# Four buffers instead of three for the weights, and sums over partitions formed as token columns

## The chip, the cores and the metric

One core of a Trainium2 chip runs the whole network in one launch. The metric is device time in microseconds, the median of the runs. All arithmetic is fp32 in and out; products run on TensorE (PE) as fp32r, three products for each fp32 one (below).

## The reference, cut to what matters

Two mixer layers (a gated mLSTM beside a sliding-window attention, then a squared-ReLU MLP), and an NSA attention layer behind them, on 512 tokens of width 1024:

```python
for l in range(2):
    h = rmsnorm(x, norm_mix_g[l])
    x = x + mixer_block(h, ...)        # mLSTM (4 heads) + windowed attention (16 heads)
    x = x + sqrelu_mlp(rmsnorm(x, norm_mlp_g[l]), w_up[l], w_down[l])
x = rmsnorm(x, final_norm_g)
u = rms_norm(x, pre_norm_gain)
x = x + rms_norm(nsa_mixer(u, ...), post_norm_gain)   # compressed, selected, windowed branch

def rmsnorm(x, g):
    y = x * lax.rsqrt(jnp.mean(x * x, axis=-1, keepdims=True) + EPS)
    return y * g
```

Every norm needs, for each token, a sum over the 1024 features. The mLSTM needs two such sums for each head (the denominator and the squares of the numerator), and the running maximum of its gates on all 128 partitions.

## The kernel before

Activations lie with features on the 128 partitions and tokens along the row, in eight tiles of 128x512. A product of the network is `gemm`: one 128x1024 weight tile of 512 KB, split into a high part `wh` and a low part `wl`, times eight pairs `xgh`, `xgl`; that is 24 matmuls of 512 columns (`mm3`: high by high, low by high, high by low). `gemm_tok` (tile `gt`) does the same with tokens on the output's partitions.

`wload` brings a weight tile: SyncE (SP) issues the DMA into `raw`, ScalarE (ACT) copies it to `wh`, VectorE (DVE) subtracts to get `wl`; in the NSA part GpSimd (POOL) does every second subtraction. `RB` buffers stand for `raw`, `WB` for each of `wh` and `wl`: three each. All other 128x512 tiles come from one pool of `U_SLOTS` = 79.

The code doesn't run in the order in which it is written. A `Recorder` notes every operation, and `issue` puts them in order with a list scheduler: it goes through time with a price for every operation (`cost`, and `load` for PE's weight loads), gives out buffers as they come free, and takes the earliest ready operation on each engine. The engines then run their queues strictly in that order. All operations are emitted from one helper line, L346, so that rows of the profile are told apart by their tiles' names.

Sums over partitions are made by `col_sums` (called 13 times: five norms through `stat_sum`, or directly in `nsa`, and eight mLSTM heads). Two matmuls with a selector of two columns as the stationary operand give a 2x512 row (`sums`, PSUM tag `o`), ACT copies it to SBUF (`sr`), four small transposes turn it into token columns (`sc`, PSUM tag `a`). `rsqrt` (DVE, then a power on POOL) and `bcast` (four transposes `bc`, an ACT copy) make of it a tile that scales columns. `mlstm_gates` writes the gates' maximum as rows 0 to 3 (high) and 32 to 35 (low) of `Mr`, and each `mlstm_head` spreads its row over the partitions with one matmul of 36 partitions (`bc<-Mr,selh`).

The scheduler's order in three places is in the section on the change. PSUM has four banks of tag `g` and two each of `a` and `o`.

Of the kernel before, what the change touches and what calls it, by code (L numbers as in the profile page):

```python
# [7 lines left out]
F32 = mybir.dt.float32  # L8
F32R = mybir.dt.float32r
AF = mybir.ActivationFunctionType  # L10
# [8 lines left out]
NB = T // 128  # L19
# [27 lines left out]
PE, ACT, DVE, POOL, SP = range(5)  # L47
# [12 lines left out]
def _free(ap):  # L60
    n = 1
    for _, c in ap.ap[1:]:
        n *= c
    return n


def _psum(ap):
    return "PSUM" in str(ap.space)
# [16 lines left out]
class Recorder:  # L85
# [14 lines left out]
    @staticmethod  # L100
    def cost(eng, name, out, wide, scalars, kw):

        n = _free(out)
        if eng == PE:
            return n * 0.4428 * (4 if name == "matmul" and wide[0].dtype == F32 else 1), False
        if eng == ACT:
            return 192 + 0.842 * n - (22 if _psum(wide[0]) else 0) + 88 * min(scalars, 2), False
        if eng == DVE:
            both = sum(1 for x in wide if not _psum(x)) > 1
            if name == "tensor_reduce":  # L110
                n = _free(wide[0])
            if name == "reciprocal":
                return 140 + 8 * n, both
            if name == "tensor_tensor_scan":
                return 1209, both
            if name in ("tensor_copy", "tensor_scalar") and not _psum(wide[0]):
                return 150 + n / 1.92 + 60 * scalars, n > 4
            return 148 + 1.05 * n + 60 * scalars, both
        if eng == POOL:
            if name == "memset":  # L120
                return 100 + 0.8 * n, False
            if kw.get("op") == ALU.pow:
                return 230 + 197 * n, True
            return (100 if name == "tensor_copy" else 170) + 2.2 * n, True
        return 60, False
# [26 lines left out]
    def add(self, eng, name, fn, args, kw):  # L152
        op = Op()
        op.eng, op.fn, op.args, op.kw, op.dma = eng, fn, args, kw, name == "dma_start"
        aps = [x for x in args if isinstance(x, bass.AP)]
        outs = [kw["out"]] if "out" in kw else [aps.pop(0)]
        ins = aps + [v for k, v in kw.items() if isinstance(v, bass.AP) and k not in ("out", "accum_out")]
        out = outs[0]
        wide = [x for x in ins if _free(x) > 1 or _free(out) == 1]
        single = [x for x in ins if not (_free(x) > 1 or _free(out) == 1)]  # L160
        op.cost, op.port = self.cost(eng, name, out, wide, len(single), kw) if not op.dma else (60, False)
        op.load = 0.8333 * _free(ins[0]) if eng == PE else 0
        op.acc = kw.get("accum_out") is not None
        op.reads = op.writes = None
        if eng in GAP:
            op.writes, op.reads = self.place(out), [self.place(x) for x in wide + single]
        if op.acc:
            outs.append(kw["accum_out"])
        i = len(self.ops)
        preds, tiles = {}, set()  # L170
        for w, ap in [(False, x) for x in ins] + [(True, x) for x in outs]:
            t, r = self.region(ap)
            if t in self.tag and self.tag[t][1]:
                tiles.add(t)
            keep, psum = [], t in self.tag and self.tag[t][0] in ("g", "a", "o")
            for q, qw, qr in self.hist.setdefault(t, []):
                hit = r is None or qr is None or (r[0] < qr[1] and qr[0] < r[1] and r[2] < qr[3] and qr[2] < r[3])
                if q != i and hit and (w or qw or psum and self.ops[q].eng != eng):
                    preds[q] = preds.get(q, False) or qw
                if not (w and hit and r is not None and qr is not None and r[0] <= qr[0] and r[1] >= qr[1]  # L180
                        and r[2] <= qr[2] and r[3] >= qr[3]):
                    keep.append((q, qw, qr))
            keep.append((i, w, r))
            self.hist[t] = keep
        for t in tiles:
            if t not in self.users:
                self.users[t] = 0
                self.first.append(t)
            self.users[t] += 1
        op.preds, op.npred, op.succs, op.tiles, op.rt = preds, len(preds), [], tiles, 0  # L190
        for q in preds:
            self.ops[q].succs.append(i)
        self.ops.append(op)
# [164 lines left out]
class Net:  # L358
# [97 lines left out]
    def col_sums(self, *xs):  # L456

        z, sel = xs[0], self.ones2r
        if len(xs) == 2:
            z, sel = self.u("hz"), self.sel2  # L460
            for n, x in enumerate(xs):
                self.tt(z[n * 64:n * 64 + 64], x[:64], x[64:], ALU.add)
        zh, zl = self.split(z, None, "sq")
        rows = self.ps("o", "sums")
        self.mm(rows[:2], sel, zh, True, False)
        self.mm(rows[:2], sel, zl, False, True)
        r = self.u("sr")
        self.nc.scalar.activation(r[:2], rows[:2], AF.Copy)
        ps = self.ps("a", "sc")
        for b in range(NB):  # L470
            self.tp(ps[:, 2 * b:2 * b + 2], r[:2, b * 128:(b + 1) * 128], 2)
        return ps

    def stat_sum(self, acc):
# [36 lines left out]
    def consts(self):  # L511
        nc, a = self.nc, self.a
        c = lambda n, name, dt=F32: nc.tile(self.cp, [128, n], dt, name, name, 1)
        self.ident = c(128, "ident")
        nc.sync.dma_start(self.ident, a["ident"])
        self.jrev = c(128, "jrev")
        nc.vector.tensor_copy(rev(self.jrev[:, :]), self.ident)
        self.bc = c(48, "bc")
        nc.sync.dma_start(self.bc, bass.AP(tensor=a["brow"].tensor, offset=a["brow"].offset,
                                             ap=[[0, 128], [1, 48]]))  # L520
        self.maskn = c(128, "maskn")
        nc.sync.dma_start(self.maskn, a["maskn"])
        self.masku = c(128, "masku")
        nc.sync.dma_start(self.masku, a["masku"])
        self.ones2r = c(2, "ones2r", F32R)
        nc.gpsimd.memset(self.ones2r.bitcast(F32), 1.0)
        self.mhalf = c(16, "mhalf")
        nc.gpsimd.memset(self.mhalf, -0.5)
        self.ones4 = nc.tile(self.cp, [4, T], F32, "ones4", "ones4", 1)
        nc.gpsimd.memset(self.ones4, 1.0)  # L530
        z = c(2, "z2")
        nc.gpsimd.memset(z, 0.0)
        for n in range(2):
            nc.gpsimd.memset(z[64 * n:64 * n + 64, n:n + 1], 1.0)
        self.sel2 = c(2, "sel2", F32R)
        nc.vector.tensor_copy(self.sel2, z)

        self.selh = nc.tile(self.cp, [36, 512], F32R, "selh", "selh", 1)
        col = lambda n: self.ident[:36, n:n + 4, None].to_broadcast([36, 4, 128])
        self.tt(self.selh.rearrange("p (h c) -> p h c", h=4), col(0), col(32), ALU.add)  # L540
        self.nsink = c(32, "nsink")
        nc.vector.tensor_scalar(self.nsink, self.bc[:, :32], -1.0, None, op0=ALU.mult)
        self.gmh = c(16, "gmh")
        nc.vector.tensor_scalar(self.gmh, self.pc[:, PC_GM:PC_GM + 16], 0.5, None, op0=ALU.mult)
        self.gfp = c(8, "gfp")
        self.tt(self.gfp, self.pc[:, PC_GFIN:PC_GFIN + 8], self.pc[:, PC_PRE:PC_PRE + 8])
# [315 lines left out]
    def mlstm_gates(self, gt):  # L862


        nc = self.nc
# [5 lines left out]
        z = self.sm("z", 16)  # L871
# [20 lines left out]
        for b in range(NB):  # L892
            c = slice(b * 128, (b + 1) * 128)
# [14 lines left out]
        nc.vector.tensor_scalar(fl, pcol[:, 16:32], -1.0, 85.0, op0=ALU.mult, op1=ALU.min)  # L908
        nc.scalar.activation(fl, fl, AF.Exp)
        Mr = self.u("Mr", F32R)  # L910
        nc.gpsimd.memset(Mr[:36].bitcast(F32), 0.0)
        nc.scalar.activation(Mr[:4], M[:4], AF.Copy)
        self.tt(Mr[32:36], M[:4], Mr[:4].bitcast(F32), ALU.subtract)
        return Ac, Mr, fl
# [1 line left out]
    def mlstm_head(self, h, q, k, V, vc, gates):  # L916
        nc = self.nc
        Ac, Mr, fl = gates
        pm, nMb = self.ps("a", "bc"), self.u("nMb")
        self.mm(pm, self.selh[:, h * 128:h * 128 + 128], Mr[:36], True, True)  # L920
        nc.scalar.activation(nMb, pm, AF.Copy, scale=-1.0)
        nMd = self.u("nMd")
        self.tt(nMd.rearrange("p (b t) -> p b t", b=NB), nMb.rearrange("p (b t) -> p b t", b=NB),
# [2 lines left out]
        for j in range(NB):  # L926
            c = slice(j * 128, (j + 1) * 128)
            n = T - j * 128
            ps = self.ps("a", "ST")
# [14 lines left out]
        for v in range(2):  # L944
            o = self.ps("o", "num")
# [18 lines left out]
        r = self.rsqrt(t, 1.0 / 256)  # L964
# [395 lines left out]
        self.nsa(x_dram, xs, st[0], st[1], out)  # L1360


U_SLOTS, SM_SLOTS, WB, RB = 79, 32, 3, 3
POOL_LO, WARM, WINDOW = 2, 7, 500
RESERVE = {"u": 8, "sm": 8, "a": 99, "o": 99, "g": 99, "raw": 99, "wh": 99, "wl": 99}

# [106 lines left out]
```

## Time and profile before

| what | us |
|---|---|
| median of 3 runs | 2156.1 (2155.67 to 2156.34) |
| the profiled execution | 2155.65 |
| its span, first to last instruction | 2153.9 |
| PE matmuls busy | 2131.5 (99%) |
| PE weight loads busy (beside the matmuls) | 1776.9 (83%) |
| DVE, ACT, POOL busy | 1371.9, 1063.6, 425.2 |
| granted TensorE clock, mean over the span | 0.997 |

A matmul's end is modelled in the profile, so that a busy share says little of PE; the distance from one matmul's start to the next one's start is what it costs. Both 1.2 and 2.4 GHz occur: a granted clock of 1.00 is 2.4 GHz. "Idle" in brackets is the time in which the engine did nothing just before the instruction, with the one that ended it.

### The profile page before, as it was taken

What the parts mean: (1) busy time and instruction counts of PE and PEld (TensorE: products, weight loads), DVE (VectorE), ACT (ScalarE), POOL (GpSimd) and SP (SyncE); (2) the same over time, 40 slices, a digit from 0 to 9 for tenths busy, and PEclk for the clock granted to TensorE, in tenths of its full rate; (3) what the DMA queues carried; (4) which work ended last, traced back from release to release, by engine and by line L of the source; (5) the groups of instructions that cost most, each with busy time, mean ns of one, the idle gap of its engine ahead of it and who ended that gap; (6) DMA issues with size and microseconds to landing.
All of it is one profiled execution on the core that took longest, in us unless ns stands there. A gap on an engine that the chain in (4) does not pass through costs nothing.

```text
span 2153.9 us, 28049 instructions
## 1 busy us (share of the span) xinstructions
PE 2131.5 (99%) x10389; PEld 1776.9 (83%) x10389; DVE 1371.9 (64%) x2587; ACT 1063.6 (49%) x2066; POOL 425.2 (20%) x470
## 2 busy tenths in 40 slices
PE   8999999999999999999999999999999999999998
PEld 6888888888888888888888888888888888888877
DVE  6688995444343445668998444434435677888786
ACT  5466773234232334456675223322324457787783
POOL 3133441011000002014453002000000404232311
PEclk9999999999999999999999999999999999999999
DMA  5223223432333333322322333333333352232231
GB/s 159 83 67 99 79 84 98 127 98 89 97 98 98 98 98 118 98 79 79 99 79 79 123 104 99 96 98 98 98 99 113 108 166 89 69 81 60 86 98 40
DMA packets 72425, 206.08 MB, mean 96 GB/s; under 512 B 9760, under 2 KB 18592, under 8 KB 72288
## 3 DMA queue, kind: packets, MB, share of 16 engines
q1 hardware_dynamic: 72288, 204.30, 30.8%
q8 instruction: 81, 1.33, 0.2%
q14 instruction: 56, 0.46, 0.1%
HBM read 197.85 MB, written 6.42 MB: 95 GB/s over the span
## 4 chain that ended last, share of the span: by engine, by line
PE 94%; DVE 2%; POOL 1%; issue 1%; DMA 1%; ACT 1%; SPq 0%; DVEq 0%; POOLq 0%; ACTq 0%
PE g L346 75%; PE gt L346 5%; PE S L346 3%; PE O L346 3%; PE PT L346 2%; PE num L346 1%; PE go L346 1%; PE ST L346 1%; DVE wl L346 0%; POOL vb L346 0%; PE bc L346 0%; POOL sq L346 0%; PE sums L346 0%; DMA raw<-wn 0%; PE sc L346 0%
## 5 line engine op out<-in xcount | busy, mean ns | idle before, releaser
L346 ACT ACTIVATE wh<-raw 128x1024 fp32r<-128x1024 f32 (+2 forms) x344 | 355.5, 1034 | 757.8 <-PE g L346 573.3
L346 PE MATMUL g<-xgh,wl 128*128 128x512 f32 x1512 | 596.2, 394 | 4.2 <-DVE wl L346 2.2
L346 PE MATMUL g<-xgh,wh 128*128 128x512 f32 x1512 | 595.6, 394 | 2.4 <-ACT wh L346 1.4
L346 PE MATMUL g<-xgl,wh 128*128 128x512 f32 x1512 | 595.2, 394 | 0.4 <-DVE xgl L346 0.4
L346 DVE TENSOR_TENSOR wl<-raw,wh 128x1024 fp32r<-128x1024 f32 (+2 forms) x327 | 409.5, 1253 | 121.0 <-ACT wh L346 119.2
L346 PEld LDWEIGHTS g<-xgh,wl 128*128 128x128 f32 x1512 | 285.0, 188 | 61.2 <-DVE wl L346 3.3
L346 PEld LDWEIGHTS g<-xgh,wh 128*128 128x128 f32 x1512 | 285.1, 189 | 58.6 <-ACT wh L346 2.4
L346 PEld LDWEIGHTS g<-xgl,wh 128*128 128x128 f32 x1512 | 284.9, 188 | 56.7 <-DVE xgl L346 1.9
L346 POOL TENSOR_TENSOR sq<-sq 128x512 f32<-128x512 f32 x50 | 83.4, 1669 | 592.3 <-ACT sq L346 581.0
L346 PE MATMUL g<-hidh,wh 128*128 128x512 f32 x512 | 199.2, 389 | 0.0
L346 PE MATMUL g<-hidh,wl 128*128 128x512 f32 x512 | 199.2, 389 | 0.0
L346 PE MATMUL g<-hidl,wh 128*128 128x512 f32 x512 | 199.2, 389 | 0.0
L346 DVE TENSOR_TENSOR x<-x,g 128x512 f32<-128x512 f32 x80 | 55.0, 688 | 207.1 <-PE g L346 207.1
L346 DVE SCALAR_TENSOR_TENSOR hz<-g,Rb 128x512 f32<-128x512 f32 x64 | 44.3, 692 | 157.8 <-PE g L346 151.8
L346 ACT ACTIVATE L<-L,mn 128x256 f32<-128x256 f32 (+3 forms) x256 | 131.2, 513 | 24.2 <-DVE mn L346 22.1
L346 PEld LDWEIGHTS g<-hidl,wh 128*128 128x128 f32 x512 | 96.1, 188 | 20.0
L346 PEld LDWEIGHTS g<-hidh,wl 128*128 128x128 f32 x512 | 96.1, 188 | 19.9
L346 PEld LDWEIGHTS g<-hidh,wh 128*128 128x128 f32 x512 | 96.1, 188 | 19.9
L346 DVE TENSOR_TENSOR pl<-PT,ph 128x512 fp32r<-128x512 f32 (+1 forms) x160 | 78.8, 525 | 22.7 <-ACT ph L346 22.0
L346 PE MATMUL gt<-wh,xgh 128*128 128x512 f32 (+3 forms) x256 | 87.8, 344 | 0.0
L346 PE MATMUL gt<-wh,xgl 128*128 128x512 f32 (+3 forms) x256 | 87.5, 342 | 0.0
L346 PE MATMUL gt<-wl,xgh 128*128 128x512 f32 (+3 forms) x256 | 87.3, 343 | 0.0
(307 smaller groups left out, 3698.2 us busy)
## 6 DMA issues: line engine op xcount, KB each, us to landing
raw<-wf SPq DMA_DIRECT2D x258, 512.0 KB, 3.5
raw<-wn SPq DMA_DIRECT2D x41, 512.0 KB, 3.7
raw<-wmv SPq DMA_DIRECT2D x16, 512.0 KB, 3.7
x<-x SPq DMA_DIRECT2D x16, 256.0 KB, 4.0
bt<-E SPq DMA_DIRECT2D x16, 256.0 KB, 5.1
xsp<-x SPq DMA_DIRECT2D x16, 256.0 KB, 2.0
raw<-w SPq DMA_DIRECT2D x8, 512.0 KB, 4.0
bn<-E SPq DMA_DIRECT2D x16, 256.0 KB, 4.9
```

The costliest lines, as they stand in the source:

```text
L346: op.fn(*op.args, **op.kw)
```

## The change

- `WB` and `RB` go from 3 to 4, `U_SLOTS` from 79 to 80. The room comes from the scratch for dynamic DMAs at the start of SBUF, which is set to 1024 bytes per partition.
- `col_sums` takes the data as the stationary operand: four 128x128 blocks of the high part, then four of the low part, each with the two-column selector as the moving operand, accumulated straight into token columns (`sums<-sel2,sqh`, PSUM tag `a`). The row in SBUF and the small transposes are gone.
- `selh` and `Mr` have 128 partitions in place of 36, the new rows being zero.
- The scheduler's price for a transpose becomes 0.844 ns per column (0.4428), and 0.42 ns for its weight load (0.8333).

```diff
-            return n * 0.4428 * (4 if name == "matmul" and wide[0].dtype == F32 else 1), False
+            return n * (0.844 if name == "transpose" else 0.4428 if wide[0].dtype == F32R else 1.771), False
...
-        op.load = 0.8333 * _free(ins[0]) if eng == PE else 0
+        op.load = (0.42 if name == "transpose" else 0.8333) * _free(ins[0]) if eng == PE else 0
...
-        zh, zl = self.split(z, None, "sq")
-        rows = self.ps("o", "sums")
-        self.mm(rows[:2], sel, zh, True, False)
-        self.mm(rows[:2], sel, zl, False, True)
-        r = self.u("sr")
-        self.nc.scalar.activation(r[:2], rows[:2], AF.Copy)
-        ps = self.ps("a", "sc")
-        for b in range(NB):
-            self.tp(ps[:, 2 * b:2 * b + 2], r[:2, b * 128:(b + 1) * 128], 2)
+        ps = self.ps("a", "sums")
+        for n, y in enumerate(self.split(z, None, "sq")):
+            for b in range(NB):
+                self.mm(ps[:, 2 * b:2 * b + 2], y[:, b * 128:(b + 1) * 128], sel, n + b == 0, n == 1)
...
-        self.selh = nc.tile(self.cp, [36, 512], F32R, "selh", "selh", 1)
-        col = lambda n: self.ident[:36, n:n + 4, None].to_broadcast([36, 4, 128])
+        self.selh = c(512, "selh", F32R)
+        col = lambda n: self.ident[:, n:n + 4, None].to_broadcast([128, 4, 128])
...
-        nc.gpsimd.memset(Mr[:36].bitcast(F32), 0.0)
+        nc.gpsimd.memset(Mr.bitcast(F32), 0.0)
...
-        self.mm(pm, self.selh[:, h * 128:h * 128 + 128], Mr[:36], True, True)
+        self.mm(pm, self.selh[:, h * 128:h * 128 + 128], Mr, True, True)
...
-U_SLOTS, SM_SLOTS, WB, RB = 79, 32, 3, 3
+U_SLOTS, SM_SLOTS, WB, RB = 80, 32, 4, 4
...
-    nc = bacc.Bacc("TRN2", target_bir_lowering=False, num_devices=1)
+    nc = bacc.Bacc("TRN2", target_bir_lowering=False, num_devices=1, dynamic_dma_scratch_size=1024)
```

Buffers and prices both feed the scheduler, so the whole order changes. Three places. The numbers behind the names are buffers' and differ between the two kernels.

PE's queue in the first layer, at the first sum over partitions, before (`gt` is the token-major product for the attention's values, with one accumulator for each of four token blocks; the first `gt` of all stands 17 rows above `sums`):

```order
L346 MATMUL gt_146<-wh_153,xgl_91 128x264
L346 MATMUL gt_145<-wl_154,xgh_90 128x264
L346 MATMUL sums_131<-sqh_129,ones2r_120 2x512
L346 MATMUL gt_147<-wh_150,xgh_81 128x264
L346 MATMUL gt_147<-wh_150,xgl_82 128x264
```

The same place after:

```order
L346 MATMUL gt_146<-wh_148,xgh_87 128x264
L346 MATMUL gt_146<-wh_148,xgl_88 128x264
L346 MATMUL gt_146<-wl_149,xgh_87 128x264
L346 MATMUL sums_129<-ones2r_120,sqh_130 128x2 x4
L346 MATMUL gt_143<-wh_151,xgh_90 128x264
```

The first `gt` now stands 24 rows above the first `sums`. Before, `sums` took a bank of tag `o`, and the third block (`gt_147`, of the same tag) came only behind it.

DVE's queue at the start of the NSA layer, before (`v` and `gate` evict the finished `gt`; `wl_2922` is the low part of the weights of the key product that PE runs next):

```order
L346 SCALAR_TENSOR_TENSOR v_2858<-gt_2890,r_2853,v_2858 128x4x64
L346 TENSOR_SCALAR gate_2864<-gt_2890,r_2853 128x48
L346 TENSOR_TENSOR wl_2922<-raw_2920,wh_2921 128x1024
L346 SCALAR_TENSOR_TENSOR v_2859<-gt_2891,r_2853,v_2859 128x4x64
L346 TENSOR_SCALAR gate_2864<-gt_2891,r_2853 128x48
```

The same place after (the key product's low part is `wl_2896`):

```order
L346 TENSOR_TENSOR Z_2927<-cf_2856,pc_74 128x4x62
L346 TENSOR_TENSOR wl_2896<-raw_2894,wh_2895 128x1024
L346 TENSOR_TENSOR Z_2927<-cf_2861,pc_74 128x4x62
L346 TENSOR_TENSOR Z_2928<-cf_2856,pc_74 128x4x62
L346 SCALAR_TENSOR_TENSOR v_2830<-gt_2862,r_2827,v_2830 128x4x64
L346 TENSOR_SCALAR gate_2838<-gt_2862,r_2827 128x48
```

The subtraction for the key product stood behind three of the four evictions of `gt`, and now stands ahead of all of them.

PE's queue near the end of the NSA layer, at the scores `S` of the windowed branch of the seventh head pair, before (`g_3987` is the last gate product, the only one left):

```order
L346 MATMUL S_3838<-kl_3511,q_3632 128x384
L346 MATMUL S_3840<-kh_3510,q_3631 128x512
L346 MATMUL S_3840<-kl_3511,q_3631 128x512
L346 MATMUL S_3842<-kh_3510,q_3632 128x512
L346 MATMUL S_3842<-kl_3511,q_3632 128x512
L346 MATMUL g_3987<-xgh_2783,wh_3985 128x512
L346 MATMUL g_3987<-xgh_2783,wl_3986 128x512
```

The same scores after (`g_3914` is the gate product ahead of the last one):

```order
L346 MATMUL S_3810<-kl_3485,q_3605 128x384
L346 MATMUL g_3914<-xgh_2791,wh_3912 128x512
L346 MATMUL g_3914<-xgh_2791,wl_3913 128x512
L346 MATMUL S_3812<-kh_3484,q_3606 128x384
L346 MATMUL S_3812<-kl_3485,q_3606 128x384
L346 MATMUL g_3914<-xgl_2792,wh_3912 128x512
L346 MATMUL g_3914<-xgh_2799,wh_3912 128x512
L346 MATMUL g_3914<-xgh_2799,wl_3913 128x512
L346 MATMUL S_3814<-kh_3484,q_3605 128x512
```

Matmuls of a product whose weights are split already now stand between the scores, and the last product comes later.

## Rows read from the trace of the kernel before

**Rows 1.** The page, part 1: busy us, share of the span, instructions.
```profile
PE 2131.5 (99%) x10389; PEld 1776.9 (83%) x10389; DVE 1371.9 (64%) x2587; ACT 1063.6 (49%) x2066; POOL 425.2 (20%) x470
```
**Rows 2.** The page, part 4: the chain that ended last, by engine.
```profile
PE 94%; DVE 2%; POOL 1%; issue 1%; DMA 1%; ACT 1%; SPq 0%; DVEq 0%; POOLq 0%; ACTq 0%
```
**Rows 3.** Waits of PE's matmuls, whole span: us in total, times, longest us.
```profile
PE sums L346 <- ACT sqh L346: 3.9, 1, 3.9
...
PE g L346 <- DVE wl L346: 2.2, 2, 1.7
PE g L346 <- POOL wl L346: 2.0, 2, 1.6
...
PE O L346 <- DVE pl L346: 1.2, 3, 0.8
PE S L346 <- DVE mn L346: 1.1, 2, 0.6
```
**Rows 4.** Timeline of PE, first mLSTM head: start us, us, engine, out<-in, shape.
```profile
67.42 0.39 PE L346 MATMUL gt<-wl,xgh 128*128 128x512 f32 x1
67.73 0.50 PE L346 MATMUL bc<-Mr,selh 36*128 36x512 f32 x1
68.16 0.50 PE L346 MATMUL ST<-ch 128*128 128x512 f32 x1
68.50 0.39 PE L346 MATMUL ST<-ch,cl 128*128 128x512 f32 x1
```
**Rows 5.** Timeline of PE, sums over partitions in the first head.
```profile
84.04 0.40 PE L346 MATMUL sums<-sqh,sel 128*2 128x512 f32 x1
84.28 0.39 PE L346 MATMUL g<-xgl,wh 128*128 128x512 f32 x1
84.51 0.40 PE L346 MATMUL g<-xgh,wh 128*128 128x512 f32 x1
...
85.89 0.40 PE L346 MATMUL gt<-wl,xgh 128*128 128x512 f32 x1
86.22 0.40 PE L346 MATMUL sc<-ident,sr 2*128 2x2 f32 x4
86.56 0.50 PE L346 MATMUL gt<-wh,xgh 128*128 128x512 f32 x1
86.90 0.40 PE L346 MATMUL gt<-wh,xgl 128*128 128x512 f32 x1
```
**Rows 6.** Short matmuls with full weights: timeline rows, and the load's group (mean ns).
```profile
2064.13 0.28 PE L346 MATMUL S<-kl,q 128*128 128x128 f32 x1
2064.24 0.28 PE L346 MATMUL O<-pl,v 128*64 128x256 f32 x1
```
```profile
L346 PEld LDWEIGHTS S<-kl,q 128*128 128x128 f32 x256 | 48.5, 189 | 3.6
```
**Rows 7.** First sum over partitions: PE, POOL (timeline), and stretch with PE's clock.
```profile
28.03 0.40 PE L346 MATMUL sums<-sqh,ones2r 128*2 128x512 f32 x1 [3.87 <-ACT sqh L346]
```
```profile
20.37 6.95 POOL L346 TENSOR_TENSOR sq<-sq 128x512 f32<-128x512 f32 x3 [2.62 <-DVE sq L346]
```
```profile
28.03:33.00 4.97, 4.97 (x27) 4.47 (x28) 2.27 (x7) 0.59 (x1) 0.17 (x1) 0.66 0.02 7
```
**Rows 8.** Timeline of PE at the start of the NSA layer.
```profile
1732.80 0.51 PE L346 MATMUL g<-xgh,wl 128*128 128x512 f32 x1 [1.67 <-DVE wl L346]
...
1742.29 0.50 PE L346 MATMUL g<-xgh,wl 128*128 128x512 f32 x1 [0.55 <-DVE wl L346]
```
**Rows 9.** PE near the end (timeline), and its stretch: length, PE, PEld, DVE, ACT, POOL, clock.
```profile
2070.44 0.80 PE L346 MATMUL g<-xgh,wh 128*128 128x512 f32 x1 [1.40 <-ACT wh L346]
2072.87 0.80 PE L346 MATMUL g<-xgh,wl 128*128 128x512 f32 x1 [1.63 <-POOL wl L346]
```
```profile
2060.00:2076.00 16.00, 11.82 (x58) 8.72 (x57) 13.12 (x35) 10.22 (x29) 5.27 (x5) 0.81 0.41 137
```
**Rows 10.** DMA issues: line, engine, count, KB each, median us to landing.
```profile
raw<-wf SPq DMA_DIRECT2D x258, 512.0 KB, 3.5
```

## Prediction

> **What bounds the kernel now.** I read the busy shares first: PE is at 99%, the next engine (DVE) at 64% [rows 1]. The chain that ended last says the same, 94% of it is PE [rows 2]. So time can come from two places alone: PE work that goes, or a wait of PE that goes. Whatever ACT or DVE is spared is worth nothing unless PE waits for it. Third, therefore, the list of PE's own waits [rows 3]: the five rows come to 10.4 us of 2153.9, half a per cent, and they sit in few places: one wait of 3.9 us for the first sum over partitions, two for a weight's low part from DVE, two from POOL, five in the attention. One more, for a high part from ACT, is 1.40 [rows 9]. Then I went to those places in the timeline, and to the matmuls that the change replaces, where the start-to-start distance is the cost: a full matmul of 512 columns takes 0.23 us (84.51 less 84.28 [rows 5]).
>
> **The change part by part.** The sum is made against the profiled execution, 2155.65 us, of which 2153.9 is the span and 1.75 lies around it; the median of the runs is 0.45 us above that execution.
>
> *The broadcast with 128 partitions.* A matmul with 36 partitions stands between two full ones. From the start of the matmul ahead of it to the start of the second one behind it are 68.50 - 67.42 = 1.08 us [rows 4]. Three full matmuls would need 0.69. The part-height one thus loses 0.39: PE does not run it up against its neighbours on either side. With all rows in use it is an ordinary matmul. There are eight (four heads, two layers): 8 x 0.39 = 3.1 us. All of it lies on PE, so all of it counts. Bounds: nothing at the least (if the gap belongs to something else), 3.1 at the most.
>
> By the Trainium skill, page "TensorE: Matmul & The Clock Gate", section "LDWEIGHTS (loading the stationary operand)", a weight load's time follows the number of columns and not the contraction's rows, and a 32x128 load takes as long as a 128x128 one. By that rule more rows change nothing, and the gain would be 3.1 us smaller; the trace has the 0.39 us beside it. It is a rival below.
>
> *Sums as token columns.* Before: two matmuls of 512 columns, 0.24 to the next start for the first and 0.23 for the second, 0.47 together; and four 2-partition transposes. These show the same loss: 86.90 - 85.89 = 1.01 us for two full matmuls (0.46) and the four, so 0.55. Together 1.02 us for each sum [rows 5]. After: eight matmuls of two columns, each with a full 128x128 weight load. No row has that shape. The nearest is a score matmul of 128 columns, bound by the load that follows it: 2064.24 - 2064.13 = 0.11 us [rows 6]. Eight make 0.88. So 0.14 less for each, times 13: 1.8 us. The bounds: if the short moving side let loads run closer, no less than the 0.06 us that 128 columns take by themselves (0.23 x 128/512), 13 x (1.02 - 0.48) = 7.0 us of gain; if each load took its full recorded 0.189 us [rows 6], 13 x (1.51 - 1.02) = 6.4 us of loss. I take 0.11, because it is a spacing and not a latency and has the same stationary shape. What else goes, the ACT copy, two semaphore hops and a bank of tag `o`, shortens the way to the scale factors, but outside the first sum no row has PE waiting for it, so nothing is counted. The wider memset and selector are as long per partition as before: nothing.
>
> *The table products* of 64 partitions (`eps`) stand in three pieces in the new order, in five before. If a piece's edge costs what a part-height matmul costs [rows 4], that is 0 to 0.8 us; I take 0.4.
>
> *The first sum.* PE waits 3.87 us for it, since POOL's chain of squares ends only at 27.32 (20.37 + 6.95) and ACT's copy comes behind it [rows 7]. That chain and the DVE operations that feed it stand in the same order after, so the end stays. But PE now has 24 instead of 17 `gt` matmuls of 264 columns ahead, 7 x 0.12 (0.23 x 264/512) = 0.8 us more cover. I count 0.7. Behind the wait the granted clock is 0.66 on average for 5 us [rows 7], part of it at 1.2 GHz; I expect that again. If a wait of 3.1 us no longer did it, some 1.7 us more would go (5 x 0.34).
>
> *The fourth buffer.* Its worth is in the other waits. At the start of the NSA layer PE waits 1.67 and 0.55 us for `wl` from DVE [rows 8], each at the head of a product. The new DVE order has the first of these subtractions ahead of the evictions it stood behind, the second ahead of the preparations of the compressed values: 2.2 us gone. Near the end the stretch of 16 us has PE busy for 11.82, so 4.2 us idle [rows 9]: 1.40 for `wh` and 1.63 for `wl` of the last product, which had no buffer to be split ahead of time, and 1.1 at scores with no other work beside them (`mn`) [rows 3]. The clock there is 0.81; I put its price at 1 us, since most of the loss falls on idle time: 5.2 us in all. In the new order the earlier product's matmuls stand between those scores and the last product comes behind the transposes. Its `wl` is still POOL's, which can start only behind `wh`, so I leave 0.7 and count 4.5 gone. What it triggers: loads are issued earlier, and ACT's and DVE's conversions stand earlier in strict queues, in front of evictions and exponentials that PE may want. Outside the places named, two milliseconds of the old order have 1.2 us of waits for `pl` and a few tenths more [rows 3]; a new order of the same quality will have its own. I add 1.9: as much as that rest, and a little for each of the three places.
>
> The sum: -3.1 - 1.8 - 0.4 - 0.7 - 2.2 - 4.5 + 1.9 = -10.8 us; 2155.65 - 10.8 = 2144.85, and with the 0.45 to the median **2145.3 us**.
>
> **The rivals.**
>
> *The waits only move.* A list scheduler with rough prices makes a new order, and PE waits as long as before at other places. For it: POOL's chain ended 3.9 us later than the order allowed for, so the prices are off by such amounts. Against it: the three places are visibly repaired. Then only PE's work counts, -5.3, and the first sum's 0.7: 2156.1 - 6.0 = 2150.1.
>
> *Two columns cost a whole weight load.* Eight loads at 0.189 us: 6.4 us lost instead of 1.8 won, 2145.3 + 8.2 = 2153.5. Against it: short matmuls run at 0.11 with the same load [rows 6].
>
> *Rows do not matter.* The loss at the 36-partition matmul is then of another kind and stays: 2145.3 + 3.1 = 2148.4. Against it: the 2-partition transposes show the same gap on both sides [rows 5]. That load time depends on columns alone is the rule of the Trainium skill's page named above.
>
> *Better than forecast.* The clock stays up after the first wait and no new waits come: -1.7 - 1.9 - 0.7, so 2141; with closer short loads 2138.
>
> *Slower: conversions in front of the softmax.* With a fourth buffer a split of the next weights is ready whenever a buffer is, and ACT and DVE run it ahead of the exponentials and minima of the 32 attention passes. If PE then had no product to run, each pass would cost what the worst one of before costs, about 0.5 us for each of two score groups (1.1 us in 2 waits [rows 3]): 32 x 0.5 = 16 us, less the 12.7 gained without the term for new waits: 2156.1 + 3.3 = 2159.4. It decides from 0.4 us a pass. Against it: only one of the 32 shows such waits now, and the new order has products between the scores. The smaller DMA scratch would end on this side as well if it slowed the loads; it decides only once a 512 KB load takes longer than the 24 matmuls that use it (24 x 0.23 = 5.5 us, against 3.5 now [rows 10]).
>
> **How the numbers follow.** Forecast, 2141 to 2149: 0.55. Waits only move, about 2150: 0.18. Rows do not matter, 2148: 0.06. Better, 2138 to 2141: 0.07. Two columns cost a load, about 2153: 0.08. Slower, 2159: 0.06. The range 2139 to 2152 leaves out the slower case, most of the two-column case and the edges. The bound of 0.2%, what a measurement of this kernel can tell from no change, is 4.3 us, so "faster" is below 2151.8: the first four cases but for a few hundredths, 0.82; within: 0.12; slower: 0.06.
>
> **What would show it.** In the new profile: `bc<-Mr,selh` with 128 rows, 0.69 us from the start ahead of it to the second one behind; eight `sums` at 0.11 us each, no `sr` and no `sc<-ident,sr`; the first wait at 3.1 us, ended by `sqh` again, with a clock below 1 behind it; no wait for `wl` at the start of the NSA layer; the last product's waits near the end below 1 us together. The prediction is wrong if `sums` starts lie 0.19 us apart, if the list of PE's waits comes to 10 us again, or if rows with `mn`, `pl` or `ph` grow to several us.

## The result, and the profile after

| kernel | median, us | range of its runs | ratio to before | 95% interval |
|---|---|---|---|---|
| before, beside it | 2155.89 | 4 runs | | |
| changed | 2142.93 | 2141.58 to 2143.57 | 0.9939 | 0.9924 to 0.9953 |

The changed kernel is 13.0 us faster; 10.8 were forecast (2145.3, range 2139 to 2152). The sum is made of terms that were off in both directions, though, and one party to the gain has no term at all. Both are taken up below.

Page of the changed kernel, part 1 and the chain by engine of part 4. They answer to [rows 1] and [rows 2].

```profile
PE 2124.0 (99%) x10415; PEld 1783.6 (83%) x10415; DVE 1378.9 (64%) x2587; ACT 1051.6 (49%) x2053; POOL 434.9 (20%) x470
```
```profile
PE 97%; DVE 1%; DMA 1%; issue 1%; POOL 0%; ACT 0%; SPq 0%; DVEq 0%; POOLq 0%; ACTq 0%
```

PE's share of the chain went from 94 to 97%. Its busy time fell by 7.5 us and the span by 12.5 (2153.9 to 2141.4): part of the gain is work, part is waiting.

Waits of PE's matmuls in the changed kernel, whole span (us in total, times, longest), to be read beside [rows 3]:

```profile
PE sums L346 <- ACT sqh L346: 2.2, 1, 2.2
PE pg L346 <- DVE gate L346: 1.3, 1, 1.3
PE PT L346 <- ACT L L346: 1.1, 1, 1.1
...
PE O L346 <- ACT ph L346: 0.8, 1, 0.8
PE gt L346 <- DVE wl L346: 0.7, 1, 0.7
...
PE O L346 <- DVE pl L346: 0.5, 1, 0.5
PE g L346 <- POOL wl L346: 0.2, 1, 0.2
```

The rows of `mn` are gone, as are 1.8 of the 2.0 us for POOL's `wl` and the 2.2 us of the key product's `wl` at the start of the NSA layer. New are `pg`, `PT`, `ph`, and a `wl` ahead of the first sum. With the 1.40 us for `wh` [rows 9] the old waits named came to 11.8 us; these come to 6.8.

*The broadcast.* PE at the first head of the changed kernel (timeline), against [rows 4]:

```profile
67.48 0.40 PE L346 MATMUL gt<-wl,xgh 128*128 128x512 f32 x1
67.72 0.40 PE L346 MATMUL bc<-Mr,selh 128*128 128x512 f32 x1
67.95 0.39 PE L346 MATMUL ST<-ch 128*128 128x512 f32 x1
68.19 0.39 PE L346 MATMUL ST<-ch,cl 128*128 128x512 f32 x1
```

From 67.48 to 68.19 are 0.71 us, 1.08 before. The weight loads (PEld) show where the time lay, first of the kernel before, then of the changed one:

```profile
67.73 0.18 PEld L346 LDWEIGHTS bc<-Mr,selh 36*128 36x128 f32 x1 [0.35 <-PE gt L346]
68.16 0.19 PEld L346 LDWEIGHTS ST<-ch 128*128 128x128 f32 x1 [0.25 <-issue]
```
```profile
67.49 0.19 PEld L346 LDWEIGHTS bc<-Mr,selh 128*128 128x128 f32 x1
67.72 0.19 PEld L346 LDWEIGHTS ST<-ch 128*128 128x128 f32 x1
```

The load itself lasts nearly the same (0.18 and 0.19). With 36 rows it began at 67.73, where the `gt` matmul ahead of it had started at 67.42 [rows 4]; the full load behind it came at 68.16, also late. With 128 rows each load begins as the matmul ahead of it does, and is hidden by it. So the rule of the Trainium skill, page "TensorE: Matmul & The Clock Gate", section "LDWEIGHTS (loading the stationary operand)", agrees with these rows as far as the load's duration goes; it says nothing of when the load may begin, and that is where the 0.39 us lay. What holds the part-height load back is not shown.

*The sums.* PE at the first head (timeline), against [rows 5]:

```profile
83.50 0.39 PE L346 MATMUL g<-xgh,wl 128*128 128x512 f32 x1
83.73 0.50 PE L346 MATMUL sums<-sel,sqh 128*128 128x2 f32 x4
84.09 0.58 PE L346 MATMUL sums<-sel,sql 128*128 128x2 f32 x4
84.54 0.49 PE L346 MATMUL g<-xgl,wh 128*128 128x512 f32 x1
84.86 0.40 PE L346 MATMUL g<-xgh,wh 128*128 128x512 f32 x1
```

83.50 to 84.86 is 1.36 us; less the two full matmuls (0.45) the eight cost 0.91, where 1.02 was read before. Where the halves stand apart, the second behind other matmuls, the sum costs between 0.92 and 1.03.

*The end.* The stretch from 2055 to 2085 us, before and after (length, then busy us of PE, PEld, DVE, ACT, POOL, then the granted clock):

```profile
2055.00:2085.00 30.00, 25.82 (x141) 20.79 (x140) 24.36 (x58) 22.47 (x53) 7.19 (x7) 0.89 0.38 123
```
```profile
2055.00:2085.00 30.00, 28.98 (x164) 24.57 (x163) 27.04 (x77) 28.73 (x73) 7.65 (x7) 1.00 0.40 133
```

PE idles 1.0 us there instead of 4.2, and the clock does not fall. (The same work stands some 12 us earlier in the changed kernel; from 2042.6 to 2072.6 us it has 28.98 us busy and a clock of 1.00 as well.)

For all kernels below the same account is made: the distance from each matmul's start to the next one's, less the time that its columns take (512 in 0.227 us). What is left is waits, edges and low clock, summed by stretches (us from the start, each kernel's times scaled so that its last matmul starts at 2153.9). The scaling moves the places: the stretch 2055-2085 is 2048 to 2078 us in the trace of the kernel before and 2036 to 2066 in that of the changed one. The columns themselves take 2045.5 us with the old sums and 2039.6 with the new, whose cost is therefore nearly all in "left over": a sum stands there with 0.57 us before and 0.96 after, on average (columns 0.46 and 0.01), so each new sum adds 0.39 to its stretch while the columns lose 0.45.

| us left over in | 0-28 | 28-60 | 60-1690 | 1690-1800 | 1800-2055 | 2055-2085 | behind | all |
|---|---|---|---|---|---|---|---|---|
| before | 11.3 | 4.5 | 35.8 | 8.0 | 23.1 | 10.2 | 6.5 | 99.4 |
| changed | 10.3 | 6.1 | 36.4 | 6.6 | 23.4 | 4.1 | 5.9 | 92.8 |
| e3 buffers alone | 11.0 | 3.4 | 36.5 | 6.3 | 28.7 | 10.7 | 5.1 | 101.7 |
| e4 prices alone | 11.2 | 4.8 | 36.2 | 8.4 | 25.2 | 10.6 | 5.0 | 101.3 |
| e12 buffers and prices | 10.9 | 4.2 | 36.0 | 5.3 | 23.3 | 4.2 | 5.8 | 89.7 |
| e6 changed, three buffers | 10.4 | 5.0 | 36.3 | 10.2 | 25.4 | 11.1 | 5.0 | 103.3 |
| e11 changed, old prices | 10.4 | 5.7 | 37.1 | 7.8 | 28.6 | 10.6 | 4.8 | 105.1 |
| e7 changed, window 480 | 10.4 | 6.2 | 36.9 | 7.2 | 25.4 | 6.5 | 6.1 | 98.5 |
| e8 before, window 480 | 11.2 | 4.3 | 38.9 | 7.2 | 25.0 | 6.1 | 5.9 | 98.6 |
| e9 first sum later | 7.9 | 6.1 | 35.6 | 6.8 | 23.3 | 4.1 | 5.9 | 89.6 |
| e10 three moves | 7.8 | 6.1 | 35.6 | 5.4 | 23.1 | 4.1 | 5.8 | 87.9 |

### The profile page after: what moved, and what is told of

The parts are those of the page before. It is cut to its first block, busy times and chain, and to the rows that moved or that the text cites. A ratio compares the mean times of both kernels' runs of the same rounds, so it can differ in the third digit from the quotient of the medians.

```text
span 2141.4 us, 28212 instructions
## 1 busy us (share of the span) xinstructions
PE 2124.0 (99%) x10415; PEld 1783.6 (83%) x10415; DVE 1378.9 (64%) x2587; ACT 1051.6 (49%) x2053; POOL 434.9 (20%) x470
## 4 chain that ended last, share of the span: by engine, by line
PE 97%; DVE 1%; DMA 1%; issue 1%; POOL 0%; ACT 0%; SPq 0%; DVEq 0%; POOLq 0%; ACTq 0%
PE g L346 76%; PE gt L346 6%; PE S L346 3%; PE O L346 3%; PE PT L346 2%; PE go L346 2%; PE num L346 1%; PE ST L346 1%; DMA x<-x 0%; PE sums L346 0%; PE hid L346 0%; PE bc L346 0%; PE sct L346 0%; PE Oc L346 0%; DVE L L346 0%
## 5 line engine op out<-in xcount | busy, mean ns | idle before, releaser
L346 DVE TENSOR_TENSOR wl<-raw,wh 128x1024 fp32r<-128x1024 f32 (+2 forms) x327 | 413.8, 1267 | 114.9 <-ACT wh L346 113.8
L346 DVE TENSOR_TENSOR pl<-PT,ph 128x512 fp32r<-128x512 f32 (+1 forms) x160 | 78.2, 523 | 13.7 <-ACT ph L346 12.9
```

The source lines that it names most:

```text
L346: op.fn(*op.args, **op.kw)
```

## The experiments

### One part at a time

**The broadcast alone**, on the kernel before:

```diff
+        self.selh = c(512, "selh", F32R)
+        col = lambda n: self.ident[:, n:n + 4, None].to_broadcast([128, 4, 128])
...
+        nc.gpsimd.memset(Mr.bitcast(F32), 0.0)
...
+        self.mm(pm, self.selh[:, h * 128:h * 128 + 128], Mr, True, True)
```

> The kernel before with one edit: the gates' maximum is spread with 128 partitions in place of 36. The order on every engine is that of before. My theory: a part-height matmul costs 0.39 us more than a full one, eight of them, so 3.1 us less: 2152.8 against 2155.9, ratio 0.9986; the distance from the matmul ahead to the second one behind falls from 1.08 to 0.69 us. Rival (a load's time follows columns, rows do not matter): no change, the distance stays at 1.08.

2151.45 us against 2155.24, ratio 0.9981 (0.9972 to 0.9990): 3.8 us less, by the interval 2.2 to 6.0. The eight `bc<-Mr,selh` cost 0.25 us each instead of 0.63, read as above; 8 x 0.38 = 3.05. The rest need not be the edit's: every engine's order is that of before, but in this execution POOL's three squares took 5.22 us instead of 6.95 [rows 7], and PE waited 2.18 us for a `wl` ahead of the first sum in place of 3.87 for the sum.

**The sums alone**, on the kernel before:

```diff
+        ps = self.ps("a", "sums")
+        for n, y in enumerate(self.split(z, None, "sq")):
+            for b in range(NB):
+                self.mm(ps[:, 2 * b:2 * b + 2], y[:, b * 128:(b + 1) * 128], sel, n + b == 0, n == 1)
```

> The kernel before with one edit: sums over partitions as token columns (eight two-column matmuls). The order changes too. My theory: sums start 0.11 us apart, 0.88 instead of 1.02 us a sum, 1.8 us less over 13, and the first wait falls by about 0.7 us; with three buffers the waits near the start and the end of the NSA layer remain, so 2152 to 2155. Rival (a two-column matmul costs a whole recorded load): starts 0.19 us apart, 6.4 us more, about 2162.

2155.31, ratio 1.0000 (0.9991 to 1.0009). Inside, each sum is about 0.07 us cheaper, and the first is waited for 2.2 us instead of 3.9. But between 1690 and 1800 us 2.2 us more are left over (10.1 against 8.0). The sum that stands there is 0.4 of it; most of the rest is the clock. The stretch from 1720 to 1740 us, before and with the new sums (the clock is the last but two):

```profile
1720.00:1740.00 20.00, 18.34 (x122) 17.04 (x121) 19.97 (x37) 11.61 (x19) 0.00 (x0) 1.00 0.59 188
```
```profile
1720.00:1740.00 20.00, 17.97 (x104) 15.95 (x103) 17.86 (x32) 9.56 (x16) 0.00 (x0) 0.91 0.52 172
```

Behind waits of 1.29, 0.45 and 0.28 us for the weights, close together, the clock fell; behind the single wait of 1.67 us before [rows 8] it did not. A part whose own price was below a microsecond cannot be judged by the time of a kernel whose order it also changes.

**The buffers alone**, on the kernel before:

```diff
-U_SLOTS, SM_SLOTS, WB, RB = 79, 32, 3, 3
+U_SLOTS, SM_SLOTS, WB, RB = 80, 32, 4, 4
...
+    nc = bacc.Bacc("TRN2", target_bir_lowering=False, num_devices=1, dynamic_dma_scratch_size=1024)
```

> The kernel before with one edit: four buffers for raw, wh and wl, 80 slots, and the smaller scratch. My theory: the waits for wh and wl at the start of the NSA layer (2.2 us) and near its end (4.5 us with the clock) go, the first sum's wait of 3.9 us stays: 2155.9 - 6.7 + 1.9 for new waits = 2151. Rival (the waits only move): the list of PE's waits again comes to 10 us or more and the time is within 1 us of before. Rival (conversions stand in front of the softmax): over 2157, with several us of waits for mn, ph or pl.

2159.11, ratio 1.0018 (1.0010 to 1.0027): slower, where 2151 was expected. PE's waits (us in total, times, longest):

```profile
PE PT L346 <- ACT L L346: 4.1, 4, 1.6
...
PE g L346 <- POOL wl L346: 1.6, 2, 1.3
PE O L346 <- DVE pl L346: 1.5, 1, 1.5
PE pg L346 <- DVE gate L346: 1.3, 1, 1.3
...
PE S L346 <- DVE mn L346: 0.9, 2, 0.6
```

The two waits at the start of the NSA layer are gone as forecast. In their place stand waits for the exponentials (`L`), for `pl` and for `gate`. Near the end the last product waits for `wh` and `wl` no more, but the scores' `mn` and `L` are waited for instead, and the end is as bad as before. This is the rival "the waits only move", on its slower side.

**The scheduler's prices alone**, on the kernel before:

```diff
+            return n * (0.844 if name == "transpose" else 0.4428 if wide[0].dtype == F32R else 1.771), False
...
+        op.load = (0.42 if name == "transpose" else 0.8333) * _free(ins[0]) if eng == PE else 0
```

> The kernel before with one edit: the scheduler's price of transposes and of their loads. No work changes, the order does. My theory: nothing of the gain comes from it, 2155.9 within 2 us, with the three places' waits still in the list. Rival (the repaired places come from the new prices and not from the buffers): 2149 to 2151, and the waits at the start and near the end of the NSA layer are gone with three buffers.

2158.2, ratio 1.0010 (1.0002 to 1.0019): a little slower too, with 3.1 us in 3 waits for `L`. So the four parts alone are worth -3.8, 0, +3.9 and +3 us: they add up to +3, and together they give -13.

### Buffers and prices belong together

**Both on the kernel before** (the two diffs above, nothing else):

> The kernel before with the fourth buffer and the scheduler's new prices for transposes, and nothing else: sums and broadcast as before. Each of the two alone made the kernel slower (2159.1 and 2158.2). If the two together are what removes the waits, and PE's work is worth 3.1 us (broadcast) and 1.3 us (sums) whatever the order: 2142.9 + 4.4 = 2147.3, ratio 0.996, with the waits near 1733 us and 2070 us gone as in the changed kernel. If the order with the new sums is needed too: about 2155, ratio 1.000, with waits for L from ACT, pl from DVE or mn of several us.

2145.96 us against 2154.93, ratio 0.9956 (0.9942 to 0.9970): 9.0 us less with the old sums and the old broadcast. With PE's spared work (3.05 for the broadcast, 0.8 for the sums, as counted below) that makes 12.9 of the 13.0. The converse, **the changed kernel with one of the two taken back**: three buffers (`79, 32, 3, 3`), or the two old price lines.

> The changed kernel with three buffers for each part of the weights in place of four (79 slots); sums, broadcast and prices stay new, the scratch stays small. If the fourth buffer repairs the waits at the start and the end of the NSA layer, they come back (2.2 + 4.5 us, less what the new waits cost): about 2148 to 2150, ratio 0.996 to 0.997, with waits for wl from DVE near 1730 us and for wh and POOL's wl near 2070 us. If the gain beyond PE's work comes from the order as a whole and not from the buffer, it lands within 3 us of 2143 with other waits.

2152.77, ratio 0.9986 (0.9977 to 0.9994). The lost time comes back where the first theory has it: left over at 1690 to 1800 us 10.2, at 2055 to 2085 us 11.1. The total is 3 to 5 us worse than it allowed. The waits are the forecast kind only at the start of the NSA layer (1.42 us for `wh`, 0.28 for `wl`; behind them the clock is 0.66 from 1729 to 1734 us, which is 1.7 of the 10.2). Near the end they are others, of the list of PE's waits:

```profile
PE PT L346 <- ACT L L346: 2.8, 3, 1.2
...
PE O L346 <- DVE pl L346: 1.3, 3, 0.7
...
PE S L346 <- DVE mn L346: 0.7, 2, 0.4
```

Between 2055 and 2085 us PE waits for `L` (1.21 and 0.41), `pl` (0.73 and 0.26) and `mn` (0.39 and 0.31), and not for the last product's `wh` or `wl`, though there are three buffers again.

> The changed kernel with the scheduler's old prices for transposes: broadcast, sums and buffers stay changed. Buffers alone on the kernel before gave 3.9 us more, with 10 us of new waits in the attention (for L from ACT, pl from DVE, mn). If the new prices are what keeps those away: about 2150, ratio 0.997 (PE's 4.4 us of work spared, the buffers' new waits kept). If the fourth buffer brings its gain by itself in this order: within 3 us of 2143.

2154.44, ratio 0.9996 (0.9987 to 1.0004). Its waits are nearly those of the buffers alone (`L` 4.1 us in 4, `pl` 1.5, POOL's `wl` 1.6, `mn` 0.9): the new prices keep them away.

| | old prices | new prices |
|---|---|---|
| old sums and broadcast, three buffers | 2155.2 | 2158.2 |
| old sums and broadcast, four buffers | 2159.1 | 2146.0 |
| new sums and broadcast, three buffers | | 2152.8 |
| new sums and broadcast, four buffers | 2154.4 | 2142.9 |

Only the corner with both is fast, in either half. What it has at the end can be counted: the products of tile `g` in the last 80 us up to the last matmul's start, in the changed kernel, in that with both, then in the buffers alone and in the changed kernel with three buffers (length, PE's busy us with the number of matmuls, clock):

```profile
2054.50:2134.50 80.00, 11.66 (x40) 1.00 0.21 72
```
```profile
2057.30:2137.30 80.00, 11.63 (x40) 1.00 0.22 76
```
```profile
2069.20:2149.20 80.00, 7.20 (x24) 0.96 0.23 79
```
```profile
2065.00:2145.00 80.00, 7.19 (x24) 0.96 0.23 75
```

24 is one gate product: all that is left to run beside the last attention passes. 40 is one and two thirds. The kernel before has 24 as well, and so have the sums alone, the prices alone and the changed kernel with old prices. In the table, every kernel with 24 has over 10 us left over at 2055 to 2085, and every kernel with 39 or 40 has 4.1 to 6.5.

### How much is the order's luck

The scheduler's window, 480 instead of 500 operations, changes thousands of rows and nothing else. In the changed kernel:

```diff
-POOL_LO, WARM, WINDOW = 2, 7, 500
+POOL_LO, WARM, WINDOW = 2, 7, 480
```

> The changed kernel with one number of the scheduler's altered that has nothing to do with the change: it looks 480 instead of 500 operations ahead. PE's work is the same, the order differs in thousands of rows. If the changed kernel's 13 us belong to the change: 2142.9 within 2 us. If some of it is what one order happens to give: up to 5 us above or below, by waits above 0.25 us at other places, 13 us in all in the changed kernel.

2147.12, ratio 0.9959 (0.9946 to 0.9971): by the medians 4 us lost. The intervals just overlap; in the table 5.7 us more are left over. The end has its 40 matmuls; two new waits for `Lc` (3.5 us together) end at 1955 and 2042 us. The same edit on the kernel before:

> The kernel before with the scheduler looking 480 instead of 500 operations ahead. If orders of one quality differ by several us, it lies outside 2155.9 plus or minus 2, and its waits stand at other places than 1733 and 2070 us. If the waits of the kernel before come from three buffers, the waits for wl at the start of the NSA layer and for wh and wl at its end are there again and the time is within 2 us.

2154.87, ratio 0.9997 (0.9988 to 1.0006). The time is the same and the waits are not. With three buffers and old prices it has 39 gate matmuls in the last 80 us (the window, then the first row of PE's waits):

```profile
2066.20:2146.20 80.00, 11.19 (x39) 1.00 0.24 80
```
```profile
PE g L346 <- DVE wl L346: 3.2, 5, 1.7
```

The end is thus repaired without a fourth buffer (6.1 left over), while `wl` at the start of the NSA layer is waited for as before (1.7), and 3.1 us are lost between 60 and 1690. So the repair at the end is a matter of which order comes out, and the fourth buffer with the new prices is one way to it. The start of the NSA layer is another matter: in all five orders with three buffers (before, the sums alone, the prices alone, e6, e8) PE waits there for `wl` or `wh`, 1.1 to 1.7 us at the longest, and in all five with four (changed, the buffers alone, e7, e11, e12) it waits for `gate` instead.

### The height of the broadcast, in a fixed order

The changed kernel with 36 partitions; every row of PE's and ACT's queue is the same.

```diff
+        self.selh = nc.tile(self.cp, [36, 512], F32R, "selh", "selh", 1)
...
+        self.mm(pm, self.selh[:, h * 128:h * 128 + 128], Mr[:36], True, True)
```

> The changed kernel with the selector and the gates' rows back at 36 partitions; PE's and ACT's queues are word for word those of the changed kernel. If a part-height matmul loses 0.39 us against its neighbours, 8 x 0.39 = 3.1 us come back: 2142.9 + 3.1 = 2146.0, a ratio to the kernel before of about 0.9953, and the start ahead of bc<-Mr,selh to the second one behind it is 1.08 us again. If rows don't matter (the rival by the Trainium skill's rule): 2142.9, ratio 0.9939, and 0.69 us.

2144.85, ratio 0.9951 (0.9938 to 0.9963). The medians are 1.9 us apart, from different sets of runs, and the intervals overlap: by the times alone it is not settled. By the trace it is. From the `gt` ahead (65.59) to the second matmul behind (66.67) are 1.08 us again, and the eight cost 0.63 each, 3.05 us together. The span grew by 1.2 only, because this execution is 1.8 us ahead before the first of them (`bc<-Mr,selh` starts at 65.91, in the changed kernel at 67.72): behind the first sum's wait the clock stayed down for less time (0.74 from 30 to 35 us, 0.50 in the changed kernel).

### The first sum's wait, priced by taking it away

In the changed kernel, POOL's chain and PE's first sum (timeline), and the two stretches behind it:

```profile
20.24 6.75 POOL L346 TENSOR_TENSOR sq<-sq 128x512 f32<-128x512 f32 x3 [2.62 <-DVE sq L346]
```
```profile
27.70 0.49 PE L346 MATMUL sums<-ones2r,sqh 128*128 128x2 f32 x3 [2.18 <-ACT sqh L346]
```
```profile
25.00:30.00 5.00, 2.82 (x18) 2.61 (x17) 1.74 (x4) 1.58 (x2) 1.91 (x2) 0.83 0.77 287
30.00:35.00 5.00, 5.00 (x24) 5.00 (x25) 2.29 (x5) 0.00 (x0) 2.94 (x1) 0.50 0.60 158
```

From start to start the wait costs 2.35 us (27.70 less 25.24, less 0.12 for the matmul at 25.24), and at a clock of 0.83 and 0.50 another 0.9 + 2.5 us of full-speed time go. A pass over the finished order moves twelve rows of PE's queue and leaves the rest:

```diff
-        for op in out:
+        for op in self.later(out, SHIFT):
             op.fn(*op.args, **op.kw)
...
+        s0 = next(x for x in names if x.startswith("sums"))
+        b0 = next(x for x in names[names.index(s0):] if x.startswith("bc"))
...
+            if x in (s0, b0):
+                hold.append([shift, op])
+                continue
...
+SHIFT = 20
```

> The changed kernel with the order as it is but for twelve rows of PE's queue: the eight matmuls of the first sum and the four of the broadcast behind it stand twenty matmuls later, behind gt products that depend on neither. It prices the wait for the first sum. In the changed kernel PE waits 2.35 us there (25.24 to 27.70) and the granted clock is then 0.83, 0.50 and 0.99 in the three stretches of 5 us from 25 us on, which is 0.9 + 2.5 us of full-speed time lost. If both belong to the wait: 5.7 us less, 2137.2, ratio 0.991. If the clock's fall has another cause: 2.4 us less, 2140.5, ratio 0.993. If the gt products run ahead of their weights and wait there instead: 2142 to 2143, ratio 0.994, with new waits for wl or wh between 28 and 45 us.

2140.59, ratio 0.9930 (0.9916 to 0.9943), 2.3 us below the changed kernel (span 2138.2 against 2141.4). The same stretches, and PE's waits behind them (timeline):

```profile
25.00:30.00 5.00, 5.00 (x44) 4.99 (x43) 2.54 (x8) 1.58 (x2) 2.15 (x3) 1.00 0.81 287
30.00:35.00 5.00, 3.89 (x33) 3.67 (x33) 2.73 (x6) 1.87 (x3) 2.39 (x1) 1.00 0.55 203
```
```profile
32.44 0.65 PE L346 MATMUL bc<-ident,r 128*128 128x128 f32 x4 [1.11 <-POOL r L346]
...
39.76 0.47 PE L346 MATMUL gt<-wh,xgh 128*128 128x512 f32 x1 [1.01 <-DVE v L346]
```

With the wait gone the clock stays at 1.00, so its fall belonged to the wait. The time alone would not have said so: 2140.59 is what the second theory gave, in which the fall has another cause. Two waits of 1.1 and 1.0 us take part of the gain back: for `r` from POOL and for `v` from DVE, not for weights as the third theory had it. Start to start they cost 1.28 and 1.18: 2.35 + 3.4 - 2.5 = 3.3, where the span shows 3.2.

Two more moves in the same manner: `pg` eight matmuls later, and DVE's three preparations of the tables behind the low parts that PE waits for at 22.4 us:

```diff
+        queues[PE] = self.back(res, [x for x in map(name, res) if x.startswith("pg")][:1], 8)
+        queues[DVE] = self.back(queues[DVE], [next(x for x in dve if x.startswith(n)) for n in ("jrev", "selh", "nsink")], 3)
```

> As the run before, and two more moves by hand: the two matmuls of the gates' transposition (pg, which wait for DVE's gate) stand eight matmuls later, and DVE's three preparations at 20.6 us (jrev, selh, nsink, 2.2 us together) stand behind the three low parts of the weights that PE waits for. If each wait is only a matter of the order at its own place, the waits of 1.47 us at 1729 and of 0.84 us at 22.4 us go as well: 2.3 us below the run before, 2135 if that is 2137. If what is spared at 22 us only makes PE reach the next wait sooner: 1.5 us below the run before.

2138.28 (2137.82 to 2139.17), ratio 0.9920 (0.9906 to 0.9933): the fastest kernel of this study, 4.6 us below the changed one. The wait for `pg` is gone whole. That at 22.4 us came back as a wait for the first sum, since POOL's chain ends nearly when it did (26.65 us, 26.67 in the run before; timeline of PE):

```profile
27.37 0.61 PE L346 MATMUL sums<-ones2r,sqh 128*128 128x2 f32 x4 [0.90 <-ACT sqh L346]
```

The profiled span is 1.6 us shorter than that of the run before, the second theory's 1.5; the medians are 2.3 apart, the first theory's figure. The trace decides for the second theory: PE did reach the next wait sooner. A wait of 0.9 us left the clock at 1.00.

## Why the prediction was right, and where it was not

**The broadcast** (-3.1): 3.05 measured, the gap on both sides as read. The rival that rows do not matter falls: the load's duration does not depend on them, its beginning does.

**The sums** (-1.8): the price for each lies at 0.91 to 1.03 instead of 0.88; 0.76 us less over the twelve sums behind the first, so about 0.8 for all. The spacing between the two-column matmuls is at or below the 0.11 us taken ((84.54 - 83.73)/8 = 0.10). What the step left out is the edge to the next full matmul: 84.54 to 84.86 is 0.32 us where 0.23 is normal, and again where a sum is split into two places. The rival of 0.189 us falls.

**The table products** (-0.4): not separated from what stands around them.

**The first sum** (-0.7): the wait shrank about as forecast, 3.87 to 0.67 + 2.18 us, and `sqh` ends it. But the step counted the clock as unchanged, and in the profiled execution it stayed down longer: 0.9 + 2.5 us lost against 1.7 before. At the first head `bc<-Mr,selh` starts at 67.72 and stood at 67.73 [rows 4]: of 1.2 us forecast for all up to there (the wait, the tables, one sum), nothing was left. That is this execution's luck and not the order's. With 36 partitions, in the same order and behind the same wait, the clock cost 1.7 us, and `bc<-Mr,selh` starts at 65.91.

**The start of the NSA layer** (-2.2): both waits are gone, and the fourth buffer is what took them. `pg` waits 1.30 us for `gate` instead. The left-over time falls by 1.3 (unrounded), and one of the sums adds 0.4 there: 1.7 us for the waits, new ones included.

**The end** (-4.5): 6.1 us gone, 3.2 of them idle time. The mechanism is the one named, the earlier product's matmuls between the scores. The term that was mis-sized is the clock. It was priced at 1 us because most of its loss was to fall on idle time; but in the kernel before PE was busy for most of that time (length, busy us of PE, PEld, DVE, ACT, POOL, clock):

```profile
2070.00:2075.00 5.00, 2.93 (x8) 2.03 (x9) 4.27 (x10) 3.13 (x9) 2.35 (x1) 0.51 0.21 57
2075.00:2080.00 5.00, 5.00 (x28) 4.36 (x27) 3.52 (x7) 4.47 (x10) 0.00 (x0) 0.81 0.59 162
```

2.93 us busy at 0.51 and 5.00 at 0.81 are 1.4 + 1.0 = 2.4 us of full-speed time, all of it given back.

**New waits** (+1.9): `pg`, `PT` and `ph` (3.2 us together) are there; `pg` is counted above. In the long stretches little is left of the term: from 60 to 1690 the left-over time grew by 0.6, where eleven new sums add 4.2 and the broadcast takes 3.05, so the rest fell by 0.6; from 1800 to 2055 it grew by 0.3; behind 2085 it fell by 0.6.

Added up: -3.05 and -0.8 for PE's work, 0 for the rest up to 60 us, -0.6, -1.7, +0.3, -6.1 and -0.6 for the rest of the stretches in their order. That is -12.5, the difference of the spans. Against it the forecast of -10.8 counted 1.0 too much gain on the sums, 1.1 too much at the start and 0.5 at the start of the NSA layer, 1.6 too little at the end, and 1.9 for new waits where the remaining stretches together fell by 0.9. That the total came as near as 1.7 us is partly luck: 2.6 us of gain counted too much stand against 4.4 too little.

**The step that was missing.** The new prices are part of the change, and the prediction gives them no term: it read the places of the new order and put their repair down to the fourth buffer. At the start of the NSA layer that holds. At the end it does not: the buffer alone leaves the 24 matmuls there and costs 3.9 us in all, the prices alone cost 3, and both give -9.0. Nor did the last product's waits for `wh` and `wl` need the buffer to go: they are absent with the prices alone and with three buffers in the changed kernel, where `mn`, `L` and `pl` are waited for in their place. The forecast held because it was read off the order of the finished kernel, in which both are at work. "The waits only move" had too low a chance for any single edit: of the four that changed the order of the kernel before by themselves (sums, buffers, prices, window) none made it faster.

**What stays open.** Why the two together leave two thirds of a product more for the end was not traced through the scheduler. That the 40 matmuls are the cause there is read from ten orders that agree; no run moved them by themselves.

## What to carry to other kernels

Where a scheduler makes the order, an edit of its inputs has two effects. One is the work that it changes, which can be priced from rows; it kept its price in the orders tried here (0.25 against 0.63 us for each broadcast, 0.91 to 1.03 us for each sum). The other is a new order, which by itself cost between nothing and 4 us here, and with two edits together gained 9, whatever each edit was for. Price the first from the trace, read the second off the new order at the places where PE waits, and test parts in pairs, since parts tested alone can point the wrong way. Here a wait of 2 to 4 us on TensorE cost its length and the clock behind it; single waits of 0.9 to 1.7 us left the clock at 1.00. Moving a few rows by hand in a finished order was worth 4.6 us.

## What the runs showed of the hardware

- A weight load with 36 rows takes as long as one with 128 (0.18 and 0.19 us), but it did not start together with the matmul ahead (0.31 us later, where a full load starts within 0.01), nor the full load behind it together with the part-height matmul (0.43 us later): 0.38 us for each such matmul between full ones.
- Two-column matmuls with full 128x128 weights start 0.10 us apart, though each load is recorded with 0.19.
- Behind one and the same wait of 2.2 us for the first sum the clock's mean from 30 to 35 us was 0.50 in the changed kernel and 0.74 with 36 partitions; over the 10 us from 25 us on that is 3.4 us of full-speed time in the one and 1.7 in the other. It stayed at 1.00 behind waits of 0.9 to 1.1 us there, and behind one of 1.67 at the start of the NSA layer [rows 8], but fell behind three of 1.29, 0.45 and 0.28 close together.
- With the DMAs' scratch at 1024 bytes the most frequent 512 KB loads land as fast as before [rows 10], and the medians of the other three kinds are 3.3 to 3.9 us against 3.7 to 4.0:

```profile
raw<-wf SPq DMA_DIRECT2D x258, 512.0 KB, 3.5
```
